# Two pad tiles that move most of a decoder trunk's SBUF tiles to multiples of 512 bytes

## The chip, the core and the metric

The kernel runs on one core of one Trainium2 chip. The time is device microseconds for one execution of the whole program; medians of undisturbed runs are compared. TensorE (PE in the rows; its weight loads are PEld) multiplies, VectorE (DVE), ScalarE (ACT) and GpSimd (POOL) work elementwise, SyncE (SP) issues most DMAs.

## What is computed

A trunk of two layers on 256 tokens of width 1024, with float32 in and out:

```python
def reference(x, ...):
    h = x
    for layer in range(DEPTH):                      # DEPTH = 2
        i = layer // 2
        if layer % 2 == 0:
            h = h + even_mixer(rmsnorm(h, even_norm1[i]), even_w_in[i], ...)   # MoBA + differential attention
        else:
            h = h + odd_mixer(rmsnorm(h, odd_norm1[i]), odd_w_in[i], ...)      # dilated attention + MLA
        h = h + conv_ffn(rmsnorm(h, ffn_norm[layer]), ffn_w_in[layer], ...)
    return rmsnorm(h, final_norm)

def conv_ffn(h, w_in, conv_w, conv_b, w_out):       # D_FF = 2816
    u, g = jnp.split(h @ w_in, 2, axis=-1)
    g = depthwise_causal_conv(g, conv_w) + conv_b   # width 3
    return (gelu(g) * u) @ w_out
```

The large products keep float32 accuracy by splitting each operand into a high part (rounded to fp32r) and a low part, the rest: `x*w` becomes `hi*hi + lo*hi + hi*lo`, three fp32r matmuls.

## The kernel before

Weights come in 103 chunks of up to 1 MB in the order of the table `PLAN`. A chunk is loaded by SyncE into one of three tiles `raw` (L141), ACT rounds it into `whi` (L145), and DVE or POOL writes the rest into `wlo` (L146); `whi` and `wlo` have four buffers each (pool `wspl`). The residual stream stands in `hT`, and its high and low parts, scaled by the norm's gain, side by side in `xs`: for each of eight blocks of 128 rows, 256 columns `xh` and then 256 columns `xl`. Activations (`o`, `ug`, `qk`, `va` and so on) rotate through one pool `two` of twenty buffers of 2 KB per partition; softmax and the FFN gate use pool `work`.

Each matmul has its own weight load. A row names its operands as out<-moving,stationary: the stationary one is loaded, 128 columns; the moving one streams past it. Four forms hold nearly all of TensorE's time, all in fp32r and all issued by `mm` (L122):

- **narrow input products** (`colmajor`, `passmajor`): `pd<-xs,whi` and `pd<-xs,wlo`, 256 columns of `xs` past a weight block, in threes (hi by xh, hi by xl, lo by xh);
- **wide input products** (`product`, the FFN from its sixth column block on): for each of eight k, `pd<-xs,whi` with 512 columns (xh and xl at once), then `pd<-xs,wlo` with 256; 16 of each make one block;
- **output products** (`proj_tile`): `acc<-o,whi` and `acc<-o,wlo`, 256 columns of an activation tile past a weight block, 24 in one block;
- **turned products** (`vjob`, and `proj_tail` in the last FFN): the weight tile is the moving operand. `pv<-whi,xs` has 512 columns; `acc<-whi,o` has nine matmuls of 512 columns and six of 256 in one block of 15.

The last FFN's output blocks are cut as `TAIL` says. Attention scores, transposes and broadcasts are in plain fp32, where one matmul gives two records. The order on TensorE is the order of the code (`manual_schedule`); in the FFN loops the other engines' order is fixed too.

Tiles take their SBUF addresses in the order of pools and of first use: `consts`, `wraw`, `wspl`, `xpool`, `tmp`, `work`, `two`.

Of the kernel before, what the change touches and what calls it, by code (L numbers as in the profile page):

```python
# [21 lines left out]
F32 = mybir.dt.float32  # L22
# [79 lines left out]
def trunk(ctx, tc, x, rel_bias, small, lam_p, wpack, fin_g, onehot, addrow, tab, out):  # L102
    nc = tc.nc
    consts = ctx.enter_context(tc.tile_pool(name="consts", bufs=1))
# [4 lines left out]
    work = ctx.enter_context(tc.tile_pool(name="work", bufs=3))  # L109
    two = ctx.enter_context(tc.tile_pool(name="two", bufs=20))  # L110
    psum = ctx.enter_context(tc.tile_pool(name="psum", bufs=8, space=PSUM))
    dram = ctx.enter_context(tc.tile_pool(name="dram", bufs=1, space=DRAM))
    ctx.enter_context(tc.manual_schedule(engines={mybir.EngineType.PE}))

    def bank(name="ps"):
# [933 lines left out]
```

## Time and profile before

| what | value |
|---|---|
| median of 3 runs | 603.56 us (602.53 to 604.64) |
| the profiled execution | 605.06 us |
| its span | 603.3 us, so 1.76 us lie around the span |
| TensorE busy | 589.5 us, 98% of the span |
| VectorE, ScalarE, GpSimd busy | 73%, 58%, 17% |
| granted TensorE clock, mean | 0.998 of 2.4 GHz |

How to read it: TensorE's matmuls overlap, since each is shown until its last result is out, so the time of one record is longer than the time until the next one starts. What counts below is the distance from start to start: in the chain of work that ended last, a piece "2.83 PE acc L122 x24" is 24 matmuls in 2.83 us. The chain is followed back from the last instruction; its pieces are start, length, engine, tile, line and count.

### The profile page before, as it was taken

To read this page: it belongs to the slowest core of one execution; us is meant where nothing else is said; L and a number is where in the kernel's file an instruction comes from. 1 tells how busy PE (TensorE), PEld (TensorE's weight loads), DVE (VectorE), ACT (ScalarE), POOL (GpSimd) and SP (SyncE) were. 2 spreads that over 40 slices of the span, in tenths; PEclk is the share of its full clock that TensorE was granted. 3 is DMA by queue.
4 is the path that set the end of the run, shared out by engine and by line. 5 is a ranking of instruction groups with operands and counts; after the bars stand their busy time and mean duration, and the time that the engine had idled before them with its cause. 6 is when DMAs were issued, how large, how long until landed. Compare 5 with 4: busy or idle time off the path is not lost.

```text
span 603.3 us, 10367 instructions
## 1 busy us (share of the span) xinstructions
PE 589.5 (98%) x4078; PEld 542.6 (90%) x4078; DVE 439.8 (73%) x773; ACT 349.7 (58%) x643; POOL 102.8 (17%) x97
## 2 busy tenths in 40 slices
PE   8898999999999999999999999999999999999995
PEld 8787999999999999999999998999988888888885
DVE  5688767689877877777787894658967787777752
ACT  6548557557655666556664574736655566655632
POOL 4701122032111110111142111004211111011110
PEclk9999999999999999999999999999999999999999
DMA  8988544435555445544445434334545544554301
GB/s 271 327 311 300 194 170 155 165 108 189 193 211 210 170 179 210 184 170 162 184 174 193 157 141 140 141 140 153 216 156 209 207 165 187 210 179 174 136 1 71
DMA packets 19961, 108.77 MB, mean 180 GB/s; under 512 B 2430, under 2 KB 5448, under 8 KB 7752
## 3 DMA queue, kind: packets, MB, share of 16 engines
q1 hardware_dynamic: 16416, 104.17, 48.1%
q10 hardware_dynamic: 3336, 3.41, 1.7%
q0 software_dynamic: 160, 0.52, 0.3%
q8 instruction: 32, 0.52, 0.3%
q14 instruction: 17, 0.14, 0.1%
HBM read 107.02 MB, written 1.08 MB: 179 GB/s over the span
## 4 chain that ended last, share of the span: by engine, by line
PE 86%; DVE 4%; DMA 4%; issue 2%; ACT 1%; POOL 1%; SPq 0%; POOLq 0%; ACTq 0%; DVEq 0%
PE pd L122 49%; PE acc L122 26%; DMA raw<-in_wpack_dram 4%; PE pv L122 4%; DVE wlo L146 2%; PE pO L122 2%; PE pS L122 2%; PE puq L122 1%; DVE sc L331 1%; DVE ex L341 1%; PE pukv L122 0%; PE pT L345 0%; ACT whi L145 0%; ACT sqt L219 0%; PE pss L122 0%
## 5 line engine op out<-in xcount | busy, mean ns | idle before, releaser
L122 PE MATMUL pd<-xs,whi 128*128 128x256 f32 (+1 forms) x1312 | 329.0, 330 | 1.8 <-DVE nm L331 1.3
L122 PE MATMUL pd<-xs,wlo 128*128 128x256 f32 x928 | 256.7, 282 | 1.7 <-DVE wlo L146 1.7
L146 DVE TENSOR_TENSOR wlo<-raw,whi 128x1024 fp32r<-128x1024 f32 (+1 forms) x183 | 229.3, 1278 | 27.2 <-ACT whi L145 27.1
L122 PEld LDWEIGHTS pd<-xs,whi 128*128 128x128 f32 x1312 | 219.7, 190 | 24.9 <-DVE nm L331 1.6
L145 ACT ACTIVATE whi<-raw 128x1024 fp32r<-128x1024 f32 (+1 forms) x195 | 196.4, 1032 | 69.4 <-PE pd L122 18.2
L122 PEld LDWEIGHTS pd<-xs,wlo 128*128 128x128 f32 x928 | 174.3, 190 | 2.3 <-DVE wlo L146 2.3
L122 PE MATMUL acc<-o,whi 128*128 128x256 f32 x608 | 108.7, 281 | 0.0
L122 PEld LDWEIGHTS acc<-o,whi 128*128 128x128 f32 x608 | 92.6, 188 | 1.0 <-issue 0.2
L761 POOL TENSOR_TENSOR ge<-ge,gbuf 128x256 f32<-128x256 f32 x44 | 37.4, 852 | 290.8 <-ACT ge L760 290.8
L122 PE MATMUL acc<-o,wlo 128*128 128x256 f32 x304 | 84.7, 279 | 0.0
L865 ACT ACTIVATE lowp<-pd 128x256 f32<-128x256 f32 x68 | 25.7, 378 | 79.8 <-PE pd L122 79.8
L866 DVE TENSOR_TENSOR ug<-pd,lowp 128x256 f32<-128x256 f32 x68 | 28.6, 421 | 50.2 <-ACT lowp L865 50.2
L122 PE MATMUL acc<-whi,o 128*128 128x512 f32 (+1 forms) x220 | 58.2, 350 | 0.2 <-ACT o L766 0.2
L122 PEld LDWEIGHTS acc<-o,wlo 128*128 128x128 f32 x304 | 57.2, 188 | 0.0
L122 PEld LDWEIGHTS acc<-whi,o 128*128 128x128 f32 x220 | 38.3, 188 | 7.5 <-ACT o L766 0.7
L146 POOL TENSOR_TENSOR wlo<-raw,whi 128x1024 fp32r<-128x1024 f32 (+1 forms) x12 | 26.0, 2166 | 105.8 <-ACT whi L145 58.2
L122 PE MATMUL acc<-wlo,o 128*128 128x512 f32 (+1 forms) x110 | 38.6, 351 | 0.0
L767 DVE TENSOR_TENSOR o<-ge,o 128x256 fp32r<-128x256 f32 x44 | 19.0, 438 | 21.5 <-ACT o L766 21.5
L748 ACT ACTIVATE t<-gbuf,ccol 128x256 f32<-128x256 f32 x44 | 26.4, 601 | 12.0 <-DVE gbuf L889 10.1
L766 ACT ACTIVATE o<-ge 128x256 fp32r<-128x256 f32 x44 | 18.4, 418 | 23.1 <-POOL ge L761 23.0
L334 ACT ACTIVATE ex<-sc,nm 128x256 f32<-128x256 f32 (+1 forms) x56 | 24.8, 444 | 11.2 <-DVE nm L331 11.0
L122 PE MATMUL pv<-whi,xs 128*128 128x512 f32 x96 | 30.2, 395 | 0.0
(150 smaller groups left out, 532.5 us busy)
## 6 DMA issues: line engine op xcount, KB each, us to landing
raw<-in_wpack_dram SPq DMA_DIRECT2D x95, 1024.0 KB, 4.8
raw<-in_wpack_dram SPq DMA_DIRECT2D x8, 256.0 KB, 4.8
Tt<-btab ACTq DMA_DIRECT2D x2, 1024.0 KB, 9.8
hT<-in_x_dram SPq DMA_DIRECT2D x4, 256.0 KB, 5.0
Tt<-btab ACTq DMA_DIRECT2D x1, 512.0 KB
raw<-in_wpack_dram SPq DMA_DIRECT2D x1, 512.0 KB
fin<-in_fin_g_dram POOLq DMA_DIRECT2D x2, 256.0 KB, 4.1
out_dram<-y SPq DMA_DIRECT2D x2, 256.0 KB, 2.0
```

The lines of the kernel that those rows point to most:

```text
L122: nc.tensor.matmul(o, l, r, start=start, stop=stop, skip_group_check=True)
L145: nc.scalar.activation(hi[:, s], raw[:, s], AF.Copy)
L146: (eng or nc.vector).tensor_tensor(lo[:, s], raw[:, s], hi[:, s].bitcast(F32), op=ALU.subtract)
L331: nc.vector.tensor_tensor_reduce(out=t[:, a:b], in0=p[:, a:b], in1=rev(T, b - a), scale=-1.0, scalar=BIG, op0=ALU.add, op1=ALU.min, accum_ ...
L334: nc.scalar.activation(e[:, a:b], t[:, a:b], AF.Exp, bias=nm[:, i:i + 1], scale=-1.0, accum_out=den[:, i:i + 1])
L341: nc.vector.tensor_scalar(e[:, a:b], e[:, a:b], rd[:, i:i + 1], None, op0=ALU.mult)
L748: nc.scalar.activation(t1, g[:, 2:], AF.Identity, bias=col(f, 3), scale=col(f, 2))
L761: nc.gpsimd.tensor_tensor(ge, ge, gbuf[f % 3][:, 0, 2:], op=ALU.mult)
L766: nc.scalar.activation(o[:, 0], ge, AF.Copy)
L767: nc.vector.tensor_tensor(o[:, 1], ge, o[:, 0].bitcast(F32), op=ALU.subtract)
L865: nc.scalar.activation(lowp, p[:, S:], AF.Copy)
L866: nc.vector.tensor_tensor(t[:, i], p[:, :S], lowp, op=ALU.add)
```

## The change

The change allocates two tiles of 224 bytes per partition that nothing reads or writes:

```diff
     dram = ctx.enter_context(tc.tile_pool(name="dram", bufs=1, space=DRAM))
+    consts.tile([128, 56], F32, name="pad")
+    work.tile([128, 56], F32, name="pad", bufs=1)
     ctx.enter_context(tc.manual_schedule(engines={mybir.EngineType.PE}))
```

The first comes ahead of all constants, so that everything behind it moves by 224 bytes; the second is the first tile of `work`, so that `work` and `two` move by 448. No instruction is added, removed or moved: on all five engines the rows stand in the same order with the same waits in both programs. What changes is the address in each operand. The addresses in the built programs, by their rest:

| tiles | start before, mod 64 and mod 512 | after, mod 64 and mod 512 |
|---|---|---|
| raw, whi, wlo, hT, xs | 32 and 288 | 0 and 0 |
| pool two (o, ug, qk, va, fin and so on) | 0 and 64 | 0 and 0 |
| ex, ge, lowp | 0 and 192 | 0 and 128 |
| pt, t3 | 0 and 384 | 0 and 320 |
| sc, t1 | 32 and 352 | 32 and 32 |
| diag, r_bc, r_q | 32 and 416 | 0 and 128 |
| iot, ident, ones, mhalf | 0 and 128 | 32 and 352 |
| Tt (the bias tables) | 0 and 0 | 32 and 224 |
| gbuf, its three buffers | 0, 32, 0 and 0, 32, 64 | 32, 0, 32 and 224, 256, 288 |

All 128-column blocks of the weight tiles and all 256-column halves of `xs` and `o` begin at multiples of 512 bytes from their tile's start, so each operand of the four forms has the rest of its tile.

## Rows read from the trace of the kernel before

**Rows 1.** The page: span, busy time by engine, clock in 40 slices.

```profile
span 603.3 us, 10367 instructions
PE 589.5 (98%) x4078; PEld 542.6 (90%) x4078; DVE 439.8 (73%) x773; ACT 349.7 (58%) x643; POOL 102.8 (17%) x97
PEclk9999999999999999999999999999999999999999
```

**Rows 2.** Stretches of the span: busy time of each engine, with the columns' names.

```profile
core 0: us, PE busy (x) PEld busy (x) DVE busy (x) ACT busy (x) POOL busy (x), PEclk, DMA share, GB/s
0.00:62.00 62.00, 55.09 (x380) 49.32 (x381) 43.97 (x103) 39.38 (x80) 20.45 (x21) 1.00 0.88 304
...
153.00:295.00 142.00, 142.00 (x952) 130.75 (x951) 107.99 (x154) 82.20 (x137) 15.22 (x18) 1.00 0.52 189
...
440.00:590.00 150.00, 149.77 (x835) 129.95 (x834) 109.14 (x158) 83.27 (x141) 14.96 (x19) 1.00 0.45 162
```

**Rows 3.** The chain of work, start to first FFN: start us, length us, what.

```profile
1.63 4.71 DMA raw<-in_wpack_dram
...
8.15 6.52 DMA raw<-in_wpack_dram
...
22.68 7.39 DMA raw<-in_wpack_dram
30.15 7.00 DMA raw<-in_wpack_dram
...
99.83 1.34 PE pO L122 x12
...
115.31 8.40 PE acc L122 x72
123.72 11.52 PE pd L122 x96
...
141.43 0.43 PE psb L122 x2
...
178.60 2.83 PE acc L122 x24
181.43 5.55 PE pd L122 x32
```

**Rows 4.** The chain of work, pieces of the odd layer.

```profile
336.52 0.43 PE pkr L122 x2
336.95 1.40 PE puq L122 x12
...
367.71 5.48 PE pv L122 x24
```

**Rows 5.** The chain of work, one block of the last FFN's output.

```profile
448.60 2.81 PE acc L122 x15
```

**Rows 6.** TensorE in order of time, wide input products: start, length, operation.

```profile
233.63 0.39 PE L122 MATMUL pd<-xs,whi 128*128 128x512 f32 x1
233.86 0.28 PE L122 MATMUL pd<-xs,wlo 128*128 128x256 f32 x1
233.97 0.39 PE L122 MATMUL pd<-xs,whi 128*128 128x512 f32 x1
```

**Rows 7.** Stretches, instructions on tile pd alone: PE, PEld, DVE, ACT.

```profile
0.00:62.00 62.00, 31.53 (x240) 29.63 (x240) 3.09 (x5) 0.00 (x0) 1.00 0.88 304
62.00:603.30 541.30, 308.24 (x2000) 277.07 (x2000) 41.84 (x90) 27.90 (x73) 1.00 0.46 166
```

**Rows 8.** Groups by form: count, then busy us and mean ns.

```profile
L122 PE MATMUL pd<-xs,whi 128*128 128x512 f32 x544 | 190.5, 392 | 0.0
...
L122 PE MATMUL acc<-o,whi 128*128 128x256 f32 x608 | 108.7, 281 | 0.0
...
L122 PE MATMUL acc<-o,wlo 128*128 128x256 f32 x304 | 84.7, 279 | 0.0
...
L122 PE MATMUL pv<-whi,xs 128*128 128x512 f32 x96 | 30.2, 395 | 0.0
```

**Rows 9.** Three lines that use the gate buffers: ns min/median/max.

```profile
L748 ACT ACTIVATE t<-gbuf,ccol x44: 582/602/606, 144.3 to 584.2; 128x256 f32<-128x256 f32 x44
L889 DVE TENSOR_TENSOR gbuf<-ug,r_bc x34: 691/692/694, 162.8 to 583.4; 128x512 f32<-128x512 f32 x34
L754 DVE SCALAR_TENSOR_TENSOR t<-gbuf,ccol,t x44: 472/479/486, 145.4 to 584.8; 128x256 f32<-128x256 f32 x44
```

**Rows 10.** DMA issues: count, KB each, median us to landing.

```profile
hT<-in_x_dram SPq DMA_DIRECT2D x4, 256.0 KB, 5.0
...
fin<-in_fin_g_dram POOLq DMA_DIRECT2D x2, 256.0 KB, 4.1
```

## The prediction

> **What bounds the kernel now.** I read the page's engine lines first: TensorE is busy 589.5 of 603.3 us and its clock stands at nines throughout, the 2.4 GHz level [rows 1]. The stretches say where that is a real bound [rows 2]. In the first 62 us it is not: PE has 55 busy us, the DMA share is 0.88, and the chain there runs through four loads of weights [rows 3]. From 62 us on PE leaves no gap: 142.00 of 142 us in the first FFN, 149.77 of 150 in the last, while VectorE, the next engine, has 108 and 109 there. The chain agrees: piece follows piece on PE, and one ends where the next begins (178.60 + 2.83 = 181.43) [rows 3]. So from 62 us to the end of the last product, a nanosecond more or less from one matmul's start to the next goes into the span once for each matmul. Engines other than PE are seldom on the path there.
>
> The quantity to read is therefore the distance from start to start, by form, beside the rest of each operand's address (the table of the change). Lengths are divided by counts:
>
> - narrow input products, 11.52 us for 96: **120.0 ns** [rows 3]. Both operands stand at 32 mod 64.
> - output products, 8.40 for 72 and 2.83 for 24: 116.7 and 117.9, in the mean of kinds **117.6** [rows 3]. The moving tile `o` stands at 0 mod 64, the weights at 32. The MLA products `puq` have the same rests: 1.40 for 12, 116.7 [rows 4].
> - wide input products, 5.55 for 16 pairs: **347 ns** a pair, of which the 512 columns take 230 [rows 3, 6]. Both at 32.
> - turned products: `pv`, 5.48 for 24, **228** for 512 columns, both at 32 [rows 4]; the last FFN's output, 2.81 for nine of 512 and six of 256, with the moving weights at 32 and `o` at 0 [rows 5].
>
> Three narrow input products and three output products do the same: 256 columns, 128 weights, the pattern hi, hi, lo. They differ by 2.4 ns, and the operand whose rest differs is the moving one. That is the only place in this trace where a start address goes with a time.
>
> The distances are not at a floor. A plain fp32 record of 256 columns takes 0.43/2 = 215 ns, 0.84 for a column (`psb`) [rows 3]; fp32r streams at twice that pace, so without loss 256 columns would take about 108 and 512 about 215. A weight load with only 128 columns behind it takes 1.34/12 = 112 ns (`pO`) [rows 3]. So each fp32r matmul loses some 6 to 15 ns to something that the trace does not name, and it loses nothing at half pace: `psb`, whose moving tile is at 32 mod 64, and `pkr`, whose is at 0, both take 0.43 for two [rows 3, 4].
>
> **The change part by part.** No instruction, order or wait differs, so the sum has only prices by address.
>
> *Moving operands that come to 0 mod 64.* I take the 2.4 ns as the price of a moving operand that starts at 32 mod 64, once for each matmul. After 62 us there are 2000 matmuls on `pd` [rows 7]; 544 pairs, 1088, are wide [rows 8], so 912 are narrow: 912 x 2.4 = 2.2 us. The wide pairs: 1088 x 2.4 = 2.6 us. `pv`: 96 [rows 8] x 2.4 = 0.2 us. The last FFN's output: 22 blocks of 15, 330 x 2.4 = 0.8 us. Together **5.8 us**, all of it on the path. The 2.4 is measured on the narrow form alone, so for the other 1514 matmuls it is an extension; the lowest price there is nothing (2.2 us in all), the highest I give below as a rival.
>
> *Stationary operands.* The weights come from 32 to 0 mod 64 in all forms but the turned ones. The trace has no fp32r matmul with both operands at 0. The output block with moving weights at 32 and `o` at 0 is the other mixed case: 9 x 228 + 6 x 117.6 = 2.76 would be its time at the prices of the others, and it takes 2.81 [rows 5]; an aligned stationary operand has brought nothing there. I take zero. From below it is bounded by the floors of the paragraph above (the large rival), from above by the opposite sign that this block shows: 50 ns for 15, 3.4 ns for each matmul.
>
> *Output products* keep a moving operand at 0 mod 64 (64 mod 512 becomes 0 mod 512). I take zero for the 912 of them [rows 8]; the case in which they pay is the slower rival.
>
> *VectorE, ScalarE, GpSimd.* One row settles the most: the three gate buffers stand at 0, 32 and 64 mod 512, and 34 writes into them by turns took 691 to 694 ns, 44 reads by VectorE 472 to 486 with a median of 479, 44 by ScalarE a median of 602 [rows 9]. 32 bytes cost these engines nothing, and they have a quarter of the FFN's time to spare [rows 2]. Zero, and hidden if not; `Tt` and two of three gate buffers lose their alignment, which this covers too.
>
> *Tiles that lose it on TensorE.* `ident` and `ones` go to 32 mod 64. They serve plain fp32 alone, where the rows show no difference (0.43 twice). At most 2.4 ns for 96 transposes and ten broadcasts, 0.3 us; I take zero.
>
> *Loads.* `raw` and `hT` come to 0 mod 64 as targets. Two kinds of 256 KB have either rest: `fin` (at 0) landed in 4.1 us, `hT` (at 32) in 5.0 [rows 10], but `fin` in a stretch with half the DMA traffic [rows 2]. I put the difference down to the traffic and take zero. As a bound, 0.9/5.0 of the four loads that the chain goes through (25.6 us) [rows 3] would be 4.5 us less; a loss is bounded by nothing in the trace, and from 62 us on loads are hidden.
>
> Sum: 605.06 - 5.8 = 599.3 for the profiled execution, whose time is 1.5 us over the median of the runs. Against the median, 603.56 - 5.8 = **597.8 us**.
>
> **The rivals.**
>
> *The start within a line does not matter.* The 2.4 ns may belong to the forms (which accumulators and weight blocks follow each other) and not to the address. For it: VectorE's and ScalarE's rows, and that `pv` at 32 mod 64 is as fast as anything (228 for 512). Against it: `puq` at 0 is as fast as the output products although its loop is that of the narrow ones. The time would be 603.6. By the Trainium skill (page "SBUF — State Buffer", section "Specifications (TRN2)") a line of SBUF has 16 bytes; all tiles here start at multiples of 32 before and after, so by that rule no read touches a line more or less, and the time stays. The forms' difference of 2.4 ns speaks against it, weakly.
>
> *Slower: the two streams start in step.* The narrow products could be slow because stationary and moving operand have the same rest (288 mod 512 both), so that both reads reach their boundaries together, and the output products fast because theirs differ (288 and 64). After the change all rests are 0, and the 912 output products and 60 `puq` and `pukv` would go from 117.6 to 120: 972 x 2.4 = 2.3 us, 605.9. The rows fit this nearly as well. What speaks against it is `pv`: the same rests, and no slower than the last FFN's output, where they differ. If the latter gained as much as it stands above `pv`'s price (22 x 0.05 = 1.1 us), 604.8 would be left, no change. It decides from an output block over 2.88 us (24 x 120).
>
> *Large: the loss goes.* If the whole loss comes from starts off a line and both operands must be on one, the forms fall to their floors: narrow 912 x (120 - 112) = 7.3; wide 544 x (347 - 215 - 112) = 10.9; output 912 x 5.6 = 5.1; `pv` 96 x 13 = 1.2; the last output 22 x (2.81 - 2.61) = 4.4. Together 28.9 us, 574.7; half of it, 589. For it: no fp32r matmul here has both operands at 0 mod 64, so none disproves it. Against it: if half of the condition is met, in the output products, only 2.4 of the 12 ns go. A page states what is lost: the Trainium skill ("TensorE: Matmul & The Clock Gate", section "Back-to-back issue gap") gives N/2.4 + 2.5 ns, 109 for 256 columns and 216 for 512; by these distances, with no floor at the weight load's 112, the sum would be an estimated 6 to 7 us larger.
>
> **How the numbers follow.** A measurement of this kernel tells about 0.3%, 1.8 us, from no change. A moderate gain of 1.8 to 11 us, the forecast: 0.36. The large one, over 11 us: 0.14. No change within 0.3%, by the first rival or because gains and losses of the second cancel: 0.28. Slower: 0.22, mostly at 605.4 to 608. So faster 0.50, same 0.28, slower 0.22. The range goes from 584 (0.09 below it, the better half of the large case) to 606.5 (0.10 above); the likeliest case's own range is 593 to 601.8.
>
> **What would show it.** Right: narrow products at about 117.6 ns (96 in 11.3 us), a wide block near 5.47 us, output blocks still 2.83, the first 62 us unchanged, VectorE's L889 still at 692 ns. The first rival: all pieces as before. The second: output blocks at 2.88 and narrow ones at 120. The large one: 512 columns at 216 and wide blocks near 5.2. The prediction is wrong in kind if time moves before 62 us, or if PE gets gaps behind VectorE.

## The result and the profile after

The changed kernel takes 607.53 us in the median of four runs (607.08 to 608.61), the kernel before 603.34 in four beside it: a ratio of 1.0070 with an interval of 1.0047 to 1.0093. It is slower by 4.2 us. The forecast was 597.8, and 607.5 lies above its range. The profiled execution took 608.61 us, its span is 606.8.

The page of the changed kernel, busy time by engine (all lines of the kernel are two higher than before):

```profile
PE 593.5 (98%) x4078; PEld 544.9 (90%) x4078; DVE 440.5 (73%) x773; ACT 351.4 (58%) x643; POOL 103.4 (17%) x97
```

TensorE's busy time rose by 4.0 us from 589.5, that of the other engines by 1.7 at most, and the clock's mean is 0.997 where it was 0.998 [rows 1]. The chain of work of the changed kernel (start us, length us, engine, tile, line, count), at the places of [rows 3] and [rows 4]:

```profile
115.01 8.63 PE acc L124 x72
123.64 11.52 PE pd L124 x96
...
178.88 2.88 PE acc L124 x24
181.76 5.65 PE pd L124 x32
...
339.14 0.43 PE pkr L124 x2
339.57 1.43 PE puq L124 x12
```

The narrow input products are as they were, 11.52 us for 96, and so is plain fp32 (`pkr`, 0.43 for two). The output products went from 8.40 to 8.63 for 72 and from 2.83 to 2.88 for 24, `puq` from 1.40 to 1.43 for 12. New to me was the last `pd` piece: a wide block takes 5.65, not 5.55. The kernel before has one such block too, the first of its first FFN, with the same starts as the 5.55 of the others:

```profile
156.20 5.65 PE pd L122 x32
```

In the last FFN, the place of [rows 5], the chain goes by turns:

```profile
452.01 2.76 PE acc L124 x15
454.77 5.65 PE pd L124 x32
460.42 2.81 PE acc L124 x15
463.23 5.55 PE pd L124 x32
```

Before, these were 2.81 and 5.56, block after block. The groups by form answer [rows 9]; columns: count, then busy us and mean ns of one:

```profile
L750 ACT ACTIVATE t<-gbuf,ccol 128x256 f32<-128x256 f32 x44 | 26.4, 601 | 12.0 <-DVE gbuf L891 10.1 <-DVE gbuf L773 1.9
L891 DVE TENSOR_TENSOR gbuf<-ug,r_bc 128x512 f32<-128x512 f32 x34 | 23.5, 693 | 1.2
L756 DVE SCALAR_TENSOR_TENSOR t<-gbuf,ccol,t 128x256 f32<-128x256 f32 x44 | 20.9, 479 | 0.7 <-ACT t L750 0.7
```

601, 693 and 479 ns: two of the three buffers lost their alignment, and neither engine noticed. Where the time went follows from the starts of the same pieces in both chains:

| from the start of | to the start of | before, us | after, us | difference |
|---|---|---|---|---|
| the span | `pd` x24 after the first loads | 58.55 | 57.94 | -0.6 |
| that piece | the first FFN | 65.17 | 65.70 | +0.5 |
| the first FFN | the odd layer | 186.33 | 189.02 | +2.7 |
| the odd layer | the last FFN | 98.82 | 99.59 | +0.8 |
| the last FFN | its first output block | 31.38 | 31.41 | 0.0 |
| that block | the end of the last wide block | 142.23 | 142.55 | +0.3 |
| that end | the end of the span | 20.82 | 20.59 | -0.2 |

Together +3.5, the difference of the spans. I do not count the first row as the change's: in the profiles of the kernels below that same piece starts anywhere between 55.4 and 58.6 us, as the loads fall. Without it there are 4.1 us, which is also what the medians say. By form: the mean distance from start to start of the output products, taken over some 900 of the 912, went from 117.4 to 119.9 ns (912 x 2.5 = +2.3 us), `puq` and `pukv` give +0.2, 16 of the 17 wide blocks of the first FFN and 8 of the last pay 0.09 to 0.10 each (+2.2; the 17th had 5.65 before), and 8 blocks of the last output are 0.05 shorter (-0.4). That is +4.3, for 4.1 seen.

### The profile page after: what moved, and what is told of

It is laid out like the page before. It is cut to its first block, busy times and chain, and to the rows that moved or that the text cites. A ratio compares the mean times of both kernels' runs of the same rounds, so it can differ in the third digit from the quotient of the medians.

```text
span 606.8 us, 10367 instructions
## 1 busy us (share of the span) xinstructions
PE 593.5 (98%) x4078; PEld 544.9 (90%) x4078; DVE 440.5 (73%) x773; ACT 351.4 (58%) x643; POOL 103.4 (17%) x97
## 4 chain that ended last, share of the span: by engine, by line
PE 87%; DMA 5%; DVE 3%; ACT 1%; issue 1%; POOL 1%; SPq 0%; POOLq 0%; ACTq 0%; DVEq 0%
PE pd L124 49%; PE acc L124 27%; PE pv L124 4%; DMA raw<-in_wpack_dram 3%; DMA Tt<-btab 2%; PE pO L124 2%; PE pS L124 2%; DVE wlo L148 1%; PE puq L124 1%; DVE ex L343 1%; PE pukv L124 0%; DVE sc L333 0%; PE pT L347 0%; ACT sqt L221 0%; PE pss L124 0%
## 5 line engine op out<-in xcount | busy, mean ns | idle before, releaser
L124 PE MATMUL acc<-o,whi 128*128 128x256 f32 x608 | 110.9, 284 | 0.0
L124 PEld LDWEIGHTS acc<-o,whi 128*128 128x128 f32 x608 | 94.6, 191 | 1.1 <-issue 0.2
L124 PE MATMUL acc<-o,wlo 128*128 128x256 f32 x304 | 86.2, 283 | 0.0
```

The lines of the kernel that those rows point to most:

```text
L124: nc.tensor.matmul(o, l, r, start=start, stop=stop, skip_group_check=True)
```

## The experiments

I entered with two theories: a moving operand pays for its **own start** (the forecast), or the two operands pay for the **distance** between their starts (the slower rival). Distance here means the moving operand's start less the stationary one's, in bytes; the kernel before has 32 (mod 256) in the output products and 0 in the narrow and wide ones, the changed kernel 0 in all of them. All kernels but three, which hold streams of matmuls alone, are edits of the kernel before.

**One pad at a time.** First the one ahead of the constants:

```diff
+    consts.tile([128, 56], F32, name="pad")
```

> Only the first pad: weights, raw, hT and xs start at 0 mod 512, the activation tiles of pool two at 288. The distance between the starts of an output product's two operands is 288 mod 512, as in the kernel before; the weights' own start is that of the changed kernel. In step (only the distance between the two starts counts): output blocks of 24 stay at 2.83 us, not 2.88, and with them the wide blocks at 5.55, if those follow the phase in which the output block leaves the engine: 603.3 us. Own start (weights and xs at 0 mod 64 are what costs): output blocks 2.88, wide blocks 5.65, 607.5 us. Mixed: output 2.83 but wide 5.65, some 605.5 us.

603.22 us against 603.33, ratio 0.9995 (0.9982 to 1.0008). The chain of work:

```profile
123.01 11.52 PE pd L123 x96
...
177.89 2.83 PE acc L123 x24
180.72 5.55 PE pd L123 x32
```

Weights, raw tiles, residual and `xs` all stand at multiples of 512 bytes here, and every piece is the old one. Then the other pad alone:

```diff
+    work.tile([128, 56], F32, name="pad", bufs=1)
```

> Only the second pad: weights, raw, hT and xs stay at 288 mod 512, the tiles of pool two come to 288 too, so that all operands are in step, but 32 bytes off a multiple of 64. In step: output blocks 2.88 us and, through the phase that they leave, wide blocks 5.65: 607.5 us, although nothing is aligned. Own start: output blocks 2.83, wide 5.55, 603.3 us. Mixed (output by the distance, wide by the own start): 2.88 and 5.55, some 605.5 us.

607.8 us, ratio 1.0065 (1.0049 to 1.0082). The chain of work:

```profile
179.12 2.88 PE acc L123 x24
182.00 5.65 PE pd L123 x32
```

Nothing of the four forms is aligned here (all at 288 mod 512), and the whole loss is there, wide blocks included. So the loss comes with the distance, and alignment brings neither gain nor loss. The own-start theory fell with these two.

**TensorE alone.** A kernel with nothing but streams of matmuls, its operands shifted element by element, asks whether any other engine or a transfer has a part in it:

```diff
+STAT = (("z", 0), ("h", 8))
+MOVE = list(range(0, 32)) + [32, 40, 48, 56, 64, 72, 96, 120]
+        for s, a in STAT:
+            for b in MOVE:
+                p = psum.tile([128, 512], F32, name=label(form, s, b), tag="ps")
+                fn(p, a, b)
```

> Nothing of the trunk is computed: 240 streams of fp32r matmuls on one operand pair each, with no other engine at work. Three forms (n: 48 of 256 columns in the pattern hi, hi, lo; w: 16 pairs of 512 and 256 columns; t: 18 of 512 columns), the stationary operand 0 (z) or 32 (h) bytes past a multiple of 512, the moving one 0 to 480 bytes past it, mostly in steps of 4. In step: the time of a stream follows moving start minus stationary start and repeats after 64 bytes: n at 120 ns for equal starts and near 117.5 at 32 apart, the h row being the z row moved by 32 bytes. Own start: the time follows one operand's start alone, the z and the h row are equal by column or differ by a constant. No effect of addresses: all streams of a form within 0.5 ns, and the kernels' difference comes from the other engines.

Each stream has a tile of its own name: form (n narrow, w wide, t turned), stationary start (z for 0, h for 8 elements), and two letters that count the moving start in elements (`aa` 0, `ai` 8, `bc` 28, `bw` 48, `cm` 64, `cu` 72). The chain of work:

```profile
14.38 5.76 PE nzaa L42 x48
...
62.07 5.61 PE nzai L42 x48
...
181.20 5.50 PE nzbc L42 x48
...
216.76 5.66 PE nzbw L42 x48
...
228.54 5.76 PE nzcm L42 x48
234.52 5.61 PE nzcu L42 x48
...
299.81 5.75 PE nhai L42 x48
...
347.48 5.61 PE nhaq L42 x48
...
490.07 5.55 PE wzaa L42 x32
...
531.02 5.51 PE wzah L42 x32
```

With no other engine at work the prices of the trunk are there: 5.76/48 = 120.0 ns at distance 0, 116.9 at 32 bytes. The rows with h repeat the rows with z when both operands move by 32 bytes (`nhai` as `nzaa`, `nhaq` as `nzai`), and 64 elements on everything returns (`nzcm`, `nzcu`): the price goes by the distance, with a period of 256 bytes and not the 64 that I had expected. Within the period it runs, for narrow streams, from 113.3 ns (28 elements; 5.50 for 48, since the first ten are slower) in this set to 123 (1 element); such steady values, without a stream's first matmuls, are given below too. A turned stream has 226.7 for 512 columns at distance 0, its best in this set, and up to 240 elsewhere. A wide pair is best at 7 and 15 elements. So the time of a matmul hangs on both of its starts together, and no other engine has a part in it. That the weight load's read and the moving stream's get in each other's way is the reading that I take; no run shows the place where they would meet. The Trainium skill ("SBUF — State Buffer", section "Who interferes with whom") lists them as two independent ports and says that PE waits for no one; it speaks of engines against each other, which these streams do not test. With the starts of PE's own two reads the measured time of a matmul of 256 columns varies by 10 ns.

**A price set by hand.** If the distance is the cause, `xs` 32 bytes further makes the narrow products as fast as the output products were:

```diff
+    work.tile([128, 56], F32, name="pad", bufs=1)
+    xpool.tile([128, 8], F32, name="xpad")
     hT = xpool.tile([128, KD, S], F32, name="hT")
```

> The kernel before with 32 bytes of pad ahead of xs and 224 ahead of the activation tiles: weights stay at 288 mod 512, xs comes to 320, so that in narrow and wide input products the moving operand starts 32 bytes past the stationary one (mod 256) instead of with it; the output products keep the 32 bytes that they have before. Distance theory, by the streams measured alone (period 256 bytes): narrow 120.0 -> 116.7 ns, 912 on the path, -3.0 us; wide unchanged at 347 a pair; pv, whose moving weights then start 32 bytes behind xs, 226.7 -> 233.3, 96 on the path, +0.6 us; the last output unchanged: 603.3 - 2.4 = 600.9 us. Theory that the output products' change came from the pool two alone (its own start), with xs indifferent: 603.3 us.

600.48 against 603.93, ratio 0.9953 (0.9935 to 0.9971). The chain of work:

```profile
81.66 5.61 PE pv L123 x24
...
121.22 11.20 PE pd L123 x96
```

The narrow products went from 120.0 to 116.7 ns and `pv` from 228 to 234, each as its form's stream had it. The size is the one expected, 0.4 us off.

**What the wide block hangs on.** The wide products have distance 0 before and after, yet take 5.55 or 5.65. I put blocks of them in turn with output blocks of any distance, and filled in the map from 32 to 63 elements:

```diff
+MOVE = list(range(32, 64))
+AFTER_OUT = ((0, 0), (8, 0), (28, 0), (28, 7), (28, 15), (28, 19), (8, 7))
+AFTER_LAST = ((56, 0), (0, 0), (0, 7), (0, 15), (7, 7))
```

> Nothing of the trunk is computed. The other half of the map (stationary operand at 0, moving 128 to 252 bytes past a multiple of 512, in steps of 4; streams named by form, z and two letters), and blocks as in the two FFNs: output block (ox) and wide block (oy) in turn, four times, and last-FFN block (lx) and wide block (ly). Letters a, b, ... are pairs of distances in elements of 4 bytes: o: (0,0) (8,0) (28,0) (28,7) (28,15) (28,19) (8,7); l: (56,0) (0,0) (0,7) (0,15) (7,7). If the wide block's 5.55 or 5.65 us is the phase that the block ahead leaves behind, oya shows 5.65 (as in the changed kernel), oyb 5.55 (as before), with nothing else in the program different, and the last-FFN pair lyb turns between 5.55 and 5.65. If other engines or the buffers make the difference, oya and oyb are both 5.55. The streams alone give 5.49 for a wide block at 7 or 15 elements and 113.9 ns for a narrow matmul at 28, against 5.55 and 120 at 0; if that holds in turn, oxd is 2.73 and oyd 5.49.

Names: `ox` and `oy` are an output block and the wide block behind it, `lx` and `ly` a block of the last output and the wide one behind it; the third letter is the case in the order of the lists. The chain of work:

```profile
108.99 5.45 PE nzbw L45 x48
...
541.45 2.88 PE oxa L45 x24
544.33 5.65 PE oya L45 x32
...
592.47 2.83 PE oxb L45 x24
595.30 5.55 PE oyb L45 x32
...
819.24 2.76 PE lxb L45 x15
822.01 5.65 PE lyb L45 x32
827.66 2.81 PE lxb L45 x15
830.46 5.55 PE lyb L45 x32
```

Distances (0, 0) give the first FFN after the change, (8, 0) elements that of before (its first block at 5.65 included), and the turns 2.76, 5.65, 2.81, 5.55 are the changed kernel's last FFN to the hundredth. The same wide block with the same distance thus has two steady paces, and in these pairs the block ahead goes with the one that it falls into. One case does not fit: the last output of before, (56, 0), gave 5.65 here and takes 5.56 in the kernel; a stream's pace can depend on more than the block just ahead. At 48 elements the narrow stream settled at 113.3 ns here (`nzbw`), as low as any in the map, but the same stream with the same starts had settled at 117.8 in the first set (5.66 for 48). So one distance can have two paces even in a stream by itself, and the map gives what a distance can cost, not what it must.

**Combinations.** Distance 192 bytes (48 elements) for the output products alone:

```diff
+    work.tile([128, 40], F32, name="pad", bufs=1)
```

> The kernel before with one pad of 160 bytes ahead of the activation tiles: they come to 224 mod 512, 192 bytes past the weights (mod 256), xs stays in step with the weights. Distance theory: the streams measured alone gave 113.3 ns for a narrow pattern at 192 bytes against 116.7 at 32, so output blocks of 24 go from 2.83 us to 2.72 to 2.75, 38 blocks and 60 smaller products: -3 to -4.4 us; the last output, whose stationary tile then lies 192 bytes past the moving one (turned streams: 231 instead of 233), -0.3 us; wide blocks 5.55 or 5.65 by the phase that the new output block leaves, which the streams alone do not tell (+1.7 us for the 17 of the first FFN if 5.65). 599 to 600.5 us; 601.5 with the other phase. Own-start theory: 603.5 us.

601.62 against 602.92, ratio 0.9970 (0.9957 to 0.9983). The chain of work:

```profile
174.56 2.73 PE acc L123 x24
177.29 5.55 PE pd L123 x32
...
450.69 2.78 PE acc L123 x15
453.47 5.66 PE pd L123 x32
```

The output products came to 114 ns, 3 us for 912 of them, but the last FFN's wide blocks fell into the slow pace and took 1.7 us of it (17 x 0.10). Its output blocks, with the sign of the distance turned round, gained 0.9 (22 x 0.04). The sum, 2.2, lies in the interval of 1.0 to 2.6 us that the ratio gives. Next the same 192 bytes and `xs` 32 bytes further:

```diff
+    work.tile([128, 32], F32, name="pad", bufs=1)
+    xpool.tile([128, 8], F32, name="xpad")
```

> Both shifts: xs 32 bytes past the weights, activation tiles 192 bytes past them (mod 256). If the prices add: 600.5 (xs alone, measured) - 3 to 4.4 = 596 to 597.5 us. If the phase that one block leaves behind undoes the gain of the next, nearer to 599.

600.14, ratio 0.9942 (0.9925 to 0.9959): less than both gains together (0.9953 times 0.9970 is 0.9923). The chain of work:

```profile
151.43 2.73 PE acc L123 x24
...
159.73 2.83 PE acc L123 x24
```

The narrow products kept their gain (11.21 for 96), but of the first FFN's 17 output blocks the first took 2.73 and all others 2.82 or 2.83; the 912 have 116.3 ns in the mean, where the 192 bytes alone gave 114.0. By the matmul 2.73 and 2.83 are 113.8 and 117.9, the two paces of the streams at 48 elements. Prices by distance do not add where blocks follow each other; the best wide distance should mend that:

```diff
+    work.tile([128, 24], F32, name="pad", bufs=1)
-    xs = xpool.tile([128, KD, 2, S], F32R, name="xs")
+    xs_all = xpool.tile([128, KD * 2 * S + 16], F32R, name="xs")
+    xs = xs_all[:, 15:15 + KD * 2 * S].rearrange("p (k h s) -> p k h s", k=KD, h=2)
```

> xs 60 bytes past the weights (it begins 15 elements inside its tile, so it stands at no multiple of 32 bytes at all), activation tiles 192 bytes past them. By the streams alone: narrow 117.1 to 117.8 (912 x -2.4 = -2.2 us), wide pair 343.3 instead of 346.7 (544 x -3.4 = -1.9 us), pv 233.3 (+0.6 us), output -3 to -4.4 us: 603.5 - 7 = 596 to 597 us. If a start off every multiple of 32 bytes cost anything in itself, narrow and wide would be above 120 and 347 and the time over 600 us.

596.88, ratio 0.9901 (0.9881 to 0.9920), as expected. The chain of work:

```profile
149.50 2.74 PE acc L123 x24
...
157.74 2.83 PE acc L123 x24
```

`xs` begins 60 bytes inside its tile, at a multiple of 4 bytes only. The wide blocks are at 5.50 in both FFNs and the narrow products at 117.7; the output blocks of the first FFN go by turns, 2.74 and 2.83. So a start that is aligned to nothing costs nothing by itself, for the engines that write `xs` (ScalarE's median 494 ns against 495, VectorE's 564 against 562) as little as for TensorE.

**Setting the distance from the other side, a miss.** Each weight chunk can be shifted for its own form. I took each form's best moving distance and shifted the stationary operand by its mirror:

```diff
+        if name[2] == "i":
+            return 36 if int(name[3:]) < NARROW else 57
+        return 44 if name[1] == "0" else 15
...
+        at = shift(name)
+        splits[i] = wspl.tile([128, 2048 + 64], F32R, name="whi")[:, at:at + 2048]
+        splits[i, 1] = wspl.tile([128, 2048 + 64], F32R, name="wlo")[:, at:at + 2048]
...
+        q = tmp.tile([128, S], F32, name="r_q", bufs=1)
```

> No pads; every weight chunk begins at its own element inside tiles that are 256 bytes longer, chosen by form from the streams measured alone: narrow and output products with the moving start 112 bytes past the stationary one (mod 256), wide ones 28 bytes, the last output 28 bytes, pv in step (0). Expected on the path: narrow 120 -> 113.9 (912 x -6.1 = -5.6 us), output blocks 2.83 -> 2.75 (38 x -0.08 = -3.2 us), wide blocks 5.55 -> 5.49 (34 x -0.06 = -1.9 us), last output 2.81 -> 2.73 (22 x -0.08 = -1.7 us): -12.4 us, 591 us. ScalarE and VectorE write the chunks at starts that are multiples of 4 bytes alone; if that slows them, L145 and L146 of before (1050 and 1291 ns) show it, and the time is longer where TensorE waits for them. (r_q has one buffer instead of two, to make room.)

605.6, ratio 1.0038 (1.0023 to 1.0053), where I expected 591. (To make room, `r_q` has one buffer instead of two, here and where the chunks are shifted again below.) The chain of work:

```profile
123.92 11.50 PE pd L134 x96
...
179.02 2.88 PE acc L134 x24
181.90 5.60 PE pd L134 x32
```

The narrow products stayed at 120 ns, the output blocks went to 2.88, the wide ones to 5.60; only the last output gained, from 2.81 to 2.75. VectorE's and ScalarE's splits into the shifted tiles took as long as before, 1290 and 1049 ns against 1291 and 1050, so the cost was on TensorE again. Distance as one number is thus not the whole rule. The map from the stationary side:

```diff
+STAT = list(range(0, 32)) + [36, 44, 57]
+MOVE = (("z", 0), ("h", 8))
+AFTER_OUT = ((48, 0), (48, 8), (48, 40), (48, 15), (48, 7), (8, 8), (8, 15))
+AFTER_LAST = ((0, 8), (0, 40), (16, 8), (16, 15), (56, 8))
```

> Nothing of the trunk is computed. Streams as in the first sweep, but with the moving operand fixed at 0 and the stationary one moved, 0 to 124 bytes in steps of 4 (letters aa to bf), then 144, 176 and 228 bytes; four narrow streams more (np: stationary 176, moving 32; nq: 48 and 32; nr: 64 and 32; ns: 16 and 128); and blocks in turn as before, o: (48,0) (48,8) (48,40) (48,15) (48,7) (8,8) (8,15) and l: (0,8) (0,40) (16,8) (16,15) (56,8), distances in elements of 4 bytes. If the difference of the two starts is all that counts, down to 4 bytes, the stream with the stationary operand at a is that of the first maps at -a mod 256 (narrow: a = 144 bytes like the moving start at 112, 113.9 ns; np the same). If only steps of 32 bytes are equal for both operands, and the place of the stationary start inside 32 bytes does not act like that of the moving one, the rows agree at a = 0, 32, 64, 96 bytes alone, and a = 144 and np stand near 120, as the blocks in the kernel with shifted chunks did (2.88 us for 24).

Here the letters count the stationary start, with the moving one at 0 (`aq` 16, `bk` 36). The chain of work:

```profile
107.95 5.46 PE nzaq L45 x48
...
202.26 5.76 PE nzbk L45 x48
```

16 elements (64 bytes) give 113.8 (113.3 steady), as the moving start did at 48 in the second set; 24 give 117.3 (118.7 at 40); but 36 gives 120.0 where its mirror, 28, had 113.3. At 8, 16 and 24 elements, the steps of 32 bytes tried, the two sides mirror each other to about 1.5 ns, if 48 is taken at its better pace; between these steps the stationary start acts otherwise than the moving one. Among the blocks, (48, 8) repeats the kernel with both shifts, 2.74 once and then 2.83, and (48, 7) steadies both: 2.72 and 5.49.

**The two repairs.** Weight chunks shifted by multiples of 32 bytes only, or `xs` at 7 elements with 192 bytes for the output products:

```diff
+            return 16 if int(name[3:]) < NARROW else 0 if name[1] == "0" else 56
+        return 24 if name[1] == "0" else 8
```

> Every weight chunk begins at its own multiple of 32 bytes in tiles that are 256 bytes longer; no pads. Moving start minus stationary start, mod 256: narrow and output products 192 bytes, wide ones 0 in the first FFN and 32 in the last, the last output 0, pv 0. If multiples of 32 bytes act alike on either operand, the streams and blocks measured alone hold: narrow 120 -> 113.3 (912 x -6.7 = -6.1 us), output blocks 2.83 -> 2.73 (38 x -0.10 = -3.9 us), last output 2.81 -> 2.77 (22 x -0.04 = -0.9 us), wide blocks 5.55 as before: 603 - 11 = 592 us. If shifting the stationary start is at fault in the kernel with chunks at multiples of 4 bytes whatever the step, narrow stays near 120 and the time near 605. (r_q has one buffer instead of two, to make room.)

```diff
+    work.tile([128, 24], F32, name="pad", bufs=1)
+    xs_all = xpool.tile([128, KD * 2 * S + 16], F32R, name="xs")
+    xs = xs_all[:, 7:7 + KD * 2 * S].rearrange("p (k h s) -> p k h s", k=KD, h=2)
```

> As the kernel with xs 60 bytes and the activation tiles 192 bytes past the weights, but xs 28 bytes past them. The blocks measured alone gave, for an output block at 192 bytes in turn with a wide block, 2.83 and 2.74 by turns beside 60 bytes and 2.72 each time beside 28, wide 5.49 in both. So 17 output blocks of the first FFN come to 2.72 (from 2.78 in the mean, -1.0 us), narrow 117.7 -> 117.0 (-0.6 us), pv 233 -> 237 (96 on the path, +0.4 us): 1.2 us less than there, 595.7 us. If the phase that a block leaves is not what sets the next block, output blocks still go by turns and the time is 597.

595.14 and 595.31 against 603.77, ratios 0.9864 (0.9842 to 0.9885) and 0.9857 (0.9840 to 0.9874). The chain of work of the first:

```profile
119.37 10.91 PE pd L134 x96
...
180.83 2.75 PE acc L134 x24
183.57 5.56 PE pd L134 x32
```

and of the second:

```profile
121.08 11.24 PE pd L123 x96
...
174.71 2.72 PE acc L123 x24
177.44 5.49 PE pd L123 x32
```

The first has the best narrow products (113.6 ns), but stays 3 us behind its expectation: output blocks settle at 2.75 and not 2.73, the last FFN's at 2.79 and not 2.77, and two of the five runs of 96 narrow products take 11.30 and not 10.9, both right behind 120 output products. That is some 2 of the 3 us. The narrow distance here is 48 elements, and 11.30 for 96 is 117.7 ns, the slower of its two paces again. The second came out 0.4 us below its expectation, with all blocks in step: 2.72 and 5.49. Both beat the kernel before by 1.4% and the changed one by 2%, and the second does it with one pad and one offset.

## Why the prediction was wrong

- **What bounds the kernel: right.** From 62 us on each nanosecond between matmul starts went into the time: 4.3 us of prices, 4.1 us of span.
- **Moving operands that come to 0 mod 64, -5.8 us: the step that failed.** The 2.4 ns between narrow and output products was read as the price of the moving operand's own rest. (Over all output products the difference is 2.6: their mean is 117.4, not 117.6.) The rows had two readings, since the distance of the two operands differed as well, and I named the right one as a rival only. `xs` at 0 mod 64 gave nothing: 11.52 for 96 after the change and in the first experiment.
- **Output products, taken at zero: +2.3 us.** The slower rival had the mechanism, and its price: 972 x 2.4 = 2.3 against +2.3 and +0.2. Its test, blocks at 2.88, came true.
- **Its counter-argument was a false transfer.** `pv` with equal starts was no slower, so I gave the rival little. The streams show that each form has its own map: distance 0 is slow for 256 columns in threes (120.0 of 113.3 to 124) and the best measured for turned products in that sweep (226.7 of 226.7 to 240). A form could not speak for another.
- **Wide products in the rival, held at 5.55: +2.2 us missing.** This is why 607.5 lies over the range's end of 606.5. The step assumed that an operand pair with unchanged starts keeps its price; the blocks in turn show that it can change with the block ahead. The trace of before had a sign of it that I did not read: one wide block at 5.65 among equals at 5.55.
- **The last output: -0.8 forecast, -0.4 came**, and by luck: not from the moving operand's own start, but by turns with the wide blocks' pace.
- **No change by a rule of 16-byte lines.** For alignment it holds: the first pad alone moved nothing (0.9995). As a rule that starts do not matter it fails, with the 32 bytes of `xs` that gave 0.47%.
- **The large gain: refuted.** With both operands at 0 the narrow products are at 120.0. The Trainium skill's figures for 256 and 512 columns ("TensorE: Matmul & The Clock Gate", section "Back-to-back issue gap"), 109 and 216 ns, which the page gives for a matmul by itself, were reached by no fp32r stream here: the best are 113.3 and 226.7. The floor of 112 ns that I read from `pO` as the weight load's is not one: `pO` is plain fp32, whose 128 columns alone take some 108 at 0.84 a column. No run shows what the weight load takes by itself.
- **VectorE, ScalarE, loads, fp32: right at zero.** The gate lines, `pkr`, `psb` and `pO` are unchanged, and no gap opened on TensorE. The 0.6 us that the first stretch lost lie within the 3 us by which it varies from profile to profile.

Open stays why the period is 256 bytes, what the weight load's read and the stream's read share, and what fixes the pace into which a block or a stream falls. The experiments show dependence on distance, form and predecessor; they name no circuit.

## What to carry to other kernels

Where TensorE is the bound and each matmul loads its own weights, compare start-to-start distances of equal forms: if they differ by some per cent, shift one operand's tile by 32 to 192 bytes against the other's and read the blocks again. Rounding tiles up to an alignment is no goal, and it can put two operands in step. Choose by the whole loop and not by one form's best price, since the block ahead sets the pace of the next.

## What the runs showed of the hardware

- A fp32r matmul of 256 columns with its own weight load takes 113.3 to 124 ns in a steady stream, by where its two operands start relative to each other, modulo 256 bytes; neither is helped by a start at a multiple of 64 or 512. One distance can have more than one price: 192 bytes gave 113.3 and 117.8.
- Plain fp32, at half the pace, showed nothing of it in the few distances that it had: `pkr` took 0.43 us for two before and after, though its operands, one in pool `two` and one a constant, moved by 224 bytes against each other. `psb` took 0.43 too, but the change moves both of its operands by 224 and so does not test it.
- A sequence of equal matmuls locks into one of several steady paces, 5.55 or 5.65 us for the same 32, which can alternate from block to block for the whole of an FFN.
- A moving operand that begins 28 or 60 bytes past a multiple of 64 costs nothing by that; the stationary one's start acted like the moving one's, mirrored, at the three steps of 32 bytes tried, and otherwise between them.
